# One decoder layer on one core: norm sums partly on TensorE, paired units in another order, fifth unit's weights ahead of stores, memory keys k by k

## The chip, the cores and the metric

One core of one Trainium2 chip runs the kernel. The metric is the device time of one execution in microseconds (us), as the median of three executions. Engines are named as in the profile: PE is TensorE, DVE is VectorE, ACT is ScalarE, POOL is GpSimd, SP is SyncE (which only issues DMAs here).

## The reference, cut to what matters

```python
x = x + 0.5 * swiglu(rmsnorm(x, ffn1_norm), ffn1_w_gu, ffn1_w_down)   # FFN1
h = rmsnorm(x, mix_norm)
z = h @ w_in                     # u, v | c_q, c_kv, k_rope | q_mem | three gates
y_a = spatial_gating(u, v, ...)                        # branch A
y_b = mla(c_q, c_kv, k_rope, ...)                      # branch B, causal attention
y_c = memory_attention(q_mem, mem, mem_norm, mem_w_kv, ...)   # branch C
x = x + sum_i(sigmoid(gate_i) * (y_i @ w_branch_i)) @ w_out
x = x + 0.5 * swiglu(rmsnorm(x, ffn2_norm), ffn2_w_gu, ffn2_w_down)   # FFN2

def swiglu(x, w_gu, w_down):
    g, u = split(x @ w_gu, 2)
    return (silu(g) * u) @ w_down

def memory_attention(...):       # in it, 256 memory tokens, 4 heads of 128:
    kv = rmsnorm(mem, mem_norm) @ w_kv
    k = rmsnorm(kv[keys], k_norm); v = kv[values]
```

x has 1024 tokens of 1024 channels, the FFNs are 2816 wide, and everything is fp32.

## The kernel before, in words

All activations live with channels on the partitions and tokens on the free axis, in two halves of 512 tokens; eight chunks c of 128 channels make up the 1024 channels (`DT` is 8).

**Products.** Every fp32 product is made of three passes (`mm3`, lines 139 to 141 in the profile): operands are split into a high part (`whi` by a cast on ACT, L127) and a low part (`wlo` by a subtraction on DVE, L128), and PE runs high by high, one low by high, and the other. One product of a "unit" is four blocks j of three passes, so 12 matmuls of 128x512.

**Units of seven products.** The FFN's first layer and the gates are computed two 512-wide column blocks at a time by seven products in place of eight (class `Seven`; `SwiGLU` and `Gates` derive from it). From the activations it needs the operands `b11`, `b12`, `b21`, `b22` and their combinations `t1` to `t4`; from the weights `a11`, `a12`, `a21`, `a22` and their sums `s1` to `s4` (`sums`, four DVE additions L1229 to L1234). `weights` splits one pair of them: part "a" is a11 and a12, "s" is s2 and s1, "t" is s3 and s4, "l" is a22. In this order a unit runs a11·b11, s2·t2, a12·b21, s1·t1, s3·t3, s4·b22, a22·t4. DVE adds the results together (`add`, L1255), ACT applies silu (L1459) or sigmoid (L1407), and `gate` multiplies (L1455).

**Pairs.** Where the second half of the tokens is not yet normalized, two units f and g run together (`units`): first s3·t3 and s4·b22 of both, which need the first half alone; meanwhile the second half's norm is made; then a11·b11, a12·b21, s2·t2, s1·t1 of both and a22·t4 of each. This happens three times: at the start of FFN1 (units 1 and 2, behind a unit 0 whose products are computed row by row on raw fp32, L1498), before the gates (units 0 and 1) and in FFN2 (units 0 and 1). There PE, DVE and ACT follow the order in which the code is written (`manual_schedule`). The unit behind a pair (3 in FFN1, 2 elsewhere) and all later ones run in `unit`, where a scheduler places DVE's and ACT's instructions.

**Norms.** ACT squares a chunk (L1112, L1116 adds it up on DVE; L354 and L359 elsewhere); `token_sums` then sums over channels with matmuls of the running sum by a column of ones (L368), ten small DVE instructions take the root (`rms`, L149 to L167), and `turn` spreads it with four transposes (L380) for the DVE products of L1141 and L1145.

**Spill.** Finished hidden blocks are combined on POOL (L1589) and stored by SP's queue; the weights of unit f are fetched by SP's queue too (`fetch`), in program order with the stores.

**Memory branch.** `mem_kv` normalizes the memory tokens and makes k and v with 48 matmuls each; in between a "filler" gives PE products of branch A, 12 matmuls at a time. `head_norm` normalizes k (L657 to L663), `to_feature` transposes it (L413).

Of the kernel before, what the change touches and what calls it, by code (L numbers as in the profile page):

```python
# [8 lines left out]
F32 = mybir.dt.float32  # L9
# [7 lines left out]
P = 128  # L17
# [25 lines left out]
class Kernel:  # L43
# [82 lines left out]
    def split(self, hi, lo, src, eng=None):  # L126
        self.nc.scalar.copy(hi, src)  # L127
        return (eng or self.nc.vector).tensor_tensor(lo, src, hi.bitcast(F32), op=ALU.subtract)  # L128

# [232 lines left out]
    def token_sums(self, acc, late=False, bank=None):  # L362


        n = acc.shape[-1] // P
        b = (bank or self.bank)()[:, :n]
        for t in range(n):
            i = self.nc.tensor.matmul(  # L368
                b[:, t:t + 1], acc[:, t * P:(t + 1) * P], self.ones, start=True, stop=True)
            if late and t == 0:  # L370
                self.after(i, self.last)
        return b
# [47 lines left out]
    def latent(self, h):  # L420
# [10 lines left out]
        def c_q(hf):  # L431
            acc, cols = None, slice(hf * 512, hf * 512 + 512)
            for j, d in enumerate(cq):
# [6 lines left out]
                eps[:, hf * 4:hf * 4 + 4], self.token_sums(acc), EPS / QR, EPS * EPS, op0=ALU.mult, op1=ALU.add)  # L440
# [224 lines left out]
    def mem_kv(self, p, filler):  # L665
# [4 lines left out]
        with tc.tile_pool(name="memkv", bufs=1) as q:  # L670
# [3 lines left out]
            for _ in range(2):  # L674
                next(filler)
# [3 lines left out]
            next(filler)  # L679
            r = self.rms(self.token_sums(acc, late=True), ML // P, D)  # L680
            for _ in range(2):
                next(filler)
# [3 lines left out]
            next(filler)  # L686
            for part in range(2):
                next(filler)
                w = self.load(a["mem_w_kv"][part])
                ps = self.mm()  # L690
                for i in range(2):
                    for d in range(DT):
                        s = tuple(x[:, d, i * P:(i + 1) * P] for x in mt)
                        self.mm3(ps[:, i], s, w[d], d == 0, d == DT - 1)
                if part == 0:
                    x = q.tile([P, 2, MH, MD], F32, name="m_k")
                    self.head_norm(x, [ps[:, 0], ps[:, 1]])
                    for hh in range(0, MH, 2):
                        self.to_feature(
                            tuple(t[:, hh:hh + 2].rearrange("p h m -> p (h m)") for t in kt),  # L700
                            [x[:, t, hh + k] for k in range(2) for t in range(2)], self.mk_g,
                        )
                else:
                    self.split(vv[0], vv[1], ps)
        return kt, vv

    def mem_attention(self, h, kt, vv, filler):
# [3 lines left out]
        with tc.tile_pool(name="mematt", bufs=1) as p:  # L711
# [4 lines left out]
            nc.vector.tensor_scalar(gq, self.mq_g, -scale, None, op0=ALU.mult)  # L716
# [75 lines left out]
    def attention(self):  # L792
# [15 lines left out]
        with tc.tile_pool(name="att", bufs=1) as p:  # L808
# [3 lines left out]
            nc.vector.tensor_scalar(gq[:QK], self.g_ev["q"], -scale, None, op0=ALU.mult)  # L812
# [154 lines left out]
    def project(self, merged, norm, sink):  # L967
# [3 lines left out]
        for half in range(2):  # L971
            for c in range(DT):
# [6 lines left out]
                norm.feed(half, c)  # L979
# [17 lines left out]
    def run(self):  # L997
# [12 lines left out]
        with tc.tile_pool(name="f1", bufs=1) as fp, self.banks("f1ps") as self.pm:  # L1010
# [7 lines left out]
            ffn.up(3)  # L1018
# [7 lines left out]
            def sink(half, c):  # L1026
                add = norm.square(half, c)
                keep(x1d, rows, half, c)
                return add
# [13 lines left out]
            with tc.manual_schedule(engines={E.PE, E.SP, E.DVE, E.Activation}):  # L1043
# [7 lines left out]
                    [do(gates.turned, 1)], late)  # L1051
                gates.units((0, 1), gates.w0)
# [4 lines left out]
        with tc.tile_pool(name="f2", bufs=1) as fp, self.banks("f2ps") as self.pm:  # L1057
# [10 lines left out]
            with tc.manual_schedule(engines={E.PE, E.DVE, E.Activation}):  # L1068
                ffn.units((0, 1))
            ffn.spill(0)  # L1070
            ffn.up(2)
# [21 lines left out]
class OpNorm:  # L1093
# [7 lines left out]
    def __init__(self, k, rows, gain, scaled=False):  # L1101
        self.k, self.x, self.t, self.gain, self.scaled = k, rows, rows, gain, scaled
        self.acc, self.r, self.s, self.op, self.rows = {}, {}, {}, {}, {}

    def feed(self, half, c):
        self.acc[half] = self.k.norm_feed(self.acc.get(half), self.x(half, c), 512)

    def square(self, half, c):
# [10 lines left out]

        return add  # L1120

    def tokens(self, half):
        k = self.k
        self.s[half] = k.token_sums(self.acc.pop(half), late=k.last is not None)
# [24 lines left out]
    def put(self, name, p, src, room=None):  # L1149

        k = self.k
        hi, lo = ((room or k.h4)(F32R) for _ in range(2))
        k.split(hi, lo, src)
        self.op.setdefault(name, {})[p] = (hi, lo)

# [40 lines left out]
class Seven:  # L1196
# [9 lines left out]

    def __init__(self, k, w, pool, norm):
# [10 lines left out]
    def fetch(self, f, rooms=None):  # L1218

        t = [room() for room in rooms or [self.k.x4] * 4]  # L1220
# [4 lines left out]
    def sums(self, f):  # L1225
# [10 lines left out]
    def weights(self, f, part):  # L1236

        k = self.k
        a1, a2, sa, sb = self.quad[f]
# [607 lines left out]
```

## Time and profile before

| | us |
|---|---|
| median of three executions | 2224.83 (2224.31 to 2226.88) |
| profiled execution, its own time | 2226.85 |
| span of the profiled execution | 2224.5 |
| PE busy in it | 2192.1 (99%) |
| DVE, ACT, POOL busy | 1552.2, 895.5, 260.3 |
| mean granted PE clock | 0.997 of full speed |

The span is the time from the first to the last recorded instruction; 2.35 us of the execution's own time lie around it. PE is busy in almost all of it, so that a stage is read by the moments in which PE waits and by the granted clock.

### The profile page before, as it was taken

What the parts mean: (1) busy time and instruction counts of PE and PEld (TensorE: products, weight loads), DVE (VectorE), ACT (ScalarE), POOL (GpSimd) and SP (SyncE); (2) the same over time, 40 slices, a digit from 0 to 9 for tenths busy, and PEclk for the clock granted to TensorE, in tenths of its full rate; (3) what the DMA queues carried; (4) which work ended last, traced back from release to release, by engine and by line L of the source; (5) the groups of instructions that cost most, each with busy time, mean ns of one, the idle gap of its engine ahead of it and who ended that gap; (6) DMA issues with size and microseconds to landing.
All of it is one profiled execution on the core that took longest, in us unless ns stands there. A gap on an engine that the chain in (4) does not pass through costs nothing.

```text
span 2224.5 us, 27605 instructions
## 1 busy us (share of the span) xinstructions
PE 2192.1 (99%) x10304; PEld 1823.2 (82%) x10304; DVE 1552.2 (70%) x2408; ACT 895.5 (40%) x1498; POOL 260.3 (12%) x250
## 2 busy tenths in 40 slices
PE   9899999999999999999999999999999999999999
PEld 5678888888887888888878889988878888888887
DVE  7866666579889555467565778885886666657784
ACT  5322222243445333444344548843432222224432
POOL 0111212100000000022000131140012121210000
PEclk9999999999999999999999999999999999999999
DMA  3332323285333333225151450074033333328542
GB/s 134 105 109 100 114 100 110 87 321 192 128 113 106 123 104 123 91 78 180 42 192 48 184 227 30 29 280 192 30 118 114 100 114 100 114 94 303 180 128 104
DMA packets 113062, 285.92 MB, mean 129 GB/s; under 512 B 13344, under 2 KB 21664, under 8 KB 112800
## 3 DMA queue, kind: packets, MB, share of 16 engines
q1 hardware_dynamic: 112928, 284.16, 36.7%
q8 instruction: 81, 1.33, 0.2%
q14 instruction: 53, 0.43, 0.1%
HBM read 201.80 MB, written 82.31 MB: 128 GB/s over the span
## 4 chain that ended last, share of the span: by engine, by line
PE 87%; DVE 9%; ACT 1%; DMA 1%; issue 1%; SPq 0%; DVEq 0%; ACTq 0%
PE one L141 13%; PE one L139 13%; PE one L140 13%; PE bank L139 12%; PE bank L141 12%; PE bank L140 12%; PE mm L139 3%; PE mm L140 2%; PE mm L141 2%; DVE wlo L128 2%; PE bank L871 1%; PE bank L413 1%; DVE h L128 1%; PE bank L886 1%; PE bank L887 1%
## 5 line engine op out<-in xcount | busy, mean ns | idle before, releaser
L127 ACT CAST whi<-x 128x1024 fp32r<-128x1024 f32 (+1 forms) x193 | 181.7, 945 | 476.4 <-PE one L140 207.9
L1255 DVE TENSOR_TENSOR t<-t,one 128x512 f32<-128x512 f32 x178 | 122.3, 687 | 237.2 <-PE one L141 236.9
L128 DVE TENSOR_TENSOR wlo<-x,whi 128x1024 fp32r<-128x1024 f32 (+1 forms) x193 | 231.8, 1204 | 38.4 <-ACT whi L127 38.2
L139 PE MATMUL bank<-h,whi 128*128 128x512 f32 x644 | 251.5, 391 | 0.0
L141 PE MATMUL bank<-h,wlo 128*128 128x512 f32 x644 | 250.9, 390 | 0.5 <-DVE wlo L128 0.5
L140 PE MATMUL bank<-h,whi 128*128 128x512 f32 x644 | 251.0, 390 | 0.0
L127 ACT CAST whi<-w 128x1024 fp32r<-128x1024 f32 (+1 forms) x136 | 120.0, 898 | 169.1 <-PE one L140 66.4
L139 PE MATMUL one<-h,whi 128*128 128x512 f32 x476 | 186.0, 391 | 1.9 <-ACT t L1342 1.0
L141 PE MATMUL one<-h,wlo 128*128 128x512 f32 x476 | 185.6, 390 | 1.4 <-DVE wlo L128 1.4
L140 PE MATMUL one<-h,whi 128*128 128x512 f32 x476 | 185.2, 389 | 0.0
L128 DVE TENSOR_TENSOR wlo<-w,whi 128x1024 fp32r<-128x1024 f32 (+1 forms) x136 | 138.9, 1033 | 62.8 <-ACT whi L127 59.0
L141 PE MATMUL one<-w,wlo 128*128 128x512 f32 x392 | 153.6, 392 | 2.9 <-DVE wlo L128 2.9
L139 PE MATMUL one<-w,whi 128*128 128x512 f32 x392 | 153.6, 392 | 2.9 <-DVE t L1255 2.0
L140 PE MATMUL one<-w,whi 128*128 128x512 f32 x392 | 153.2, 391 | 0.0
L141 PEld LDWEIGHTS bank<-h,wlo 128*128 128x128 f32 x644 | 121.1, 188 | 26.2 <-DVE wlo L128 0.9
L140 PEld LDWEIGHTS bank<-h,whi 128*128 128x128 f32 x644 | 121.2, 188 | 24.9
L139 PEld LDWEIGHTS bank<-h,whi 128*128 128x128 f32 x644 | 121.2, 188 | 24.9
L1589 POOL TENSOR_TENSOR raw<-raw 128x512 f32<-128x512 f32 x42 | 69.8, 1661 | 598.3 <-DVE raw L1455 598.2
L139 PE MATMUL bank<-whi 128*128 128x512 f32 x352 | 136.9, 389 | 0.0
L140 PE MATMUL bank<-wlo,whi 128*128 128x512 f32 x352 | 136.9, 389 | 0.0
L141 PE MATMUL bank<-whi,wlo 128*128 128x512 f32 x352 | 136.9, 389 | 0.0
L1589 POOL TENSOR_TENSOR w<-raw 128x512 f32<-128x512 f32 x43 | 84.8, 1987 | 228.0 <-DVE raw L1455 228.0
(374 smaller groups left out, 4996.3 us busy)
## 6 DMA issues: line engine op xcount, KB each, us to landing
x<-in_ffn_w_gu_dram SPq DMA_DIRECT2D x78, 512.0 KB, 5.1
w<-tdt SPq DMA_DIRECT2D x40, 512.0 KB, 4.4
tdb<-raw SPq DMA_DIRECT2D x66, 256.0 KB, 2.1
h<-in_ffn_w_down_dram SPq DMA_DIRECT2D x64, 256.0 KB, 6.1
w<-tdb SPq DMA_DIRECT2D x30, 512.0 KB, 4.5
gate<-raw SPq DMA_DIRECT2D x24, 512.0 KB, 2.6
tdt<-w SPq DMA_DIRECT2D x44, 256.0 KB, 2.0
tdt<-raw SPq DMA_DIRECT2D x42, 256.0 KB, 2.8
```

The lines of the kernel that those rows point to most:

```text
L127: self.nc.scalar.copy(hi, src)
L128: return (eng or self.nc.vector).tensor_tensor(lo, src, hi.bitcast(F32), op=ALU.subtract)
L139: mmul(out, s[0], m[0], start=first, stop=False, **kw)
L140: mmul(out, s[0], m[1], start=False, stop=False, **kw)
L141: self.last = mmul(out, s[1], m[0], start=False, stop=last, **kw)
L413: nc.tensor.transpose(b[:m, k * P:(k + 1) * P], s, self.ident)
L871: nc.tensor.transpose(b[:, at:at + P], prs[t][:, kk * P:(kk + 1) * P], self.ident)
L886: nc.tensor.matmul(o, w, pt[0], start=n == 0, stop=False)
L887: nc.tensor.matmul(o, w, pt[1], start=False, stop=n == len(pts) - 1)
L1255: return self.nc.vector.tensor_tensor(out, x, y, op=ALU.add)
L1589: sub = lambda d, x, y: nc.gpsimd.tensor_tensor(d, x, y, op=ALU.subtract)
```

## The change

Six things are done.

1. `token_sums` takes a list of accumulators. Squares that are marked `plain` are no longer added up on DVE; each gets four ones-matmuls of its own. This makes 2 more accumulators for FFN1's first half (chunks 6, 7), 4 for its second (4 to 7), 2 for the gates' second half (6, 7), and 1 for FFN2's (7).
2. In `units` the token sums stand after two of the four blocks of the first product, the turn after five blocks; some weight splits move behind them; the splits of a22 and t4 are all made ahead of the last reads; both a22·t4 stand together; and the gating (`then`) comes last.
3. The next unit's "a" part and its `sums` are prepared between (`ready`), and that unit is run in the same written order (`unit(f, True)`).
4. FFN1's start is written in another order, and `fetch(4)` stands ahead of the first spill's stores.
5. `mem_kv` spreads the filler as 2, 2, 2, 2, runs each product with d outside and i inside, and has the whole v product between `head_norm` and the transposes of k.
6. Two one-column multiplications (`m_gq`, `a_gq`) go from DVE to POOL.

```diff
     def token_sums(self, accs, late=False, bank=None):
...
         for t in range(n):
+            for m, acc in enumerate(accs):
+                i = self.nc.tensor.matmul(
+                    b[:, t:t + 1], acc[:, t * P:(t + 1) * P], self.ones, start=m == 0, stop=m == len(accs) - 1)
...
             def product(w):
                 ps = self.mm()
+                for d in range(DT):
+                    for i in range(2):
                         s = tuple(x[:, d, i * P:(i + 1) * P] for x in mt)
                         self.mm3(ps[:, i], s, w[d], d == 0, d == DT - 1)
+                return ps
+
+            ps = product(self.load(a["mem_w_kv"][0]))
+            w = self.load(a["mem_w_kv"][1])
+            x = q.tile([P, 2, MH, MD], F32, name="m_k")
+            self.head_norm(x, [ps[:, 0], ps[:, 1]])
+            ps = product(w)
+            for hh in range(0, MH, 2):
+                self.to_feature(
...
+            self.product(out, w[u], s, t, js=(j,))
+            if n == 1 and not known:
+                norm.tokens(1)
+                for p in fill[0]:
+                    more(*p)
+                norm.root(1)
+                for p in fill[1]:
+                    more(*p)
+            if n == 4 and not known:
+                norm.turn(1)
...
+        for u in fs:
+            self.mark = self.add(p1[u], p1[u], z[u])
+            self.emit(u, 1, 0, p1[u], y[u])
+        for u in fs:
             self.product(y[u], w[u], "a22", "t4", False)
-            self.emit(u, 0, 0, v2, x[u], v2)
         aside()
+        for then in [self.emit(u, 0, 0, p1[u], x[u], p1[u]) for u in fs]:
+            if then:
+                then()
...
             self.units(
+                (1, 2), w, (),
+                [lambda: keep(1), lambda: self.fetch(3, [k.x4] * 2), lambda: self.ready(3)])
             finish()
+            self.fetch(4, [k.x4] * 2)
+            self.spill(0, self.w4)
+            self.hid[3] = self.w4()
+            self.unit(3, True)
+            self.spill(1)
```

PE ahead of the gates, where s3·t3 of the first gate unit (`one` by `h`) runs and the second half's norm is summed. Before:

```order
L139 MATMUL one<-h_4895,whi 128x512
L140 MATMUL one<-h_4896,whi 128x512
L141 MATMUL one<-h_4895,wlo 128x512
L368 MATMUL bank<-ones,t 128x1 x4
L139 MATMUL one<-h_4782,whi 128x512
...
L141 MATMUL one<-h_4891,wlo 128x512
L380 MATMUL bank<-ident,rs_y 128x128 x4
L139 MATMUL bank<-h_4786,whi 128x512
```

Now (h_4913 is what h_4895 was, h_4800 what h_4782 was):

```order
L144 MATMUL one<-h_4804,whi 128x512
L145 MATMUL one<-h_4805,whi 128x512
L146 MATMUL one<-h_4804,wlo 128x512
L374 MATMUL bank<-ones,t 128x1 x12
L144 MATMUL one<-h_4913,whi 128x512
...
L146 MATMUL one<-h_4800,wlo 128x512
L386 MATMUL bank<-ident,rs_y 128x128 x4
L144 MATMUL one<-h_4800,whi 128x512
```

The sums (12 matmuls where 4 stood) moved ahead of the first product's second half, and the turn from behind the second product to its middle.

ACT at the end of FFN1's pair. The pair's silus write `t` (L1459, now L1498); the casts of unit 3's weights read `x4` tiles: whi_626 and whi_657 before, whi_632 and whi_677 now, are its parts "a" and "s". L1524, now L1565, is unit 0's silu. Before:

```order
L127 CAST x4_580<-x4_146 128x1024
L1459 ACTIVATE t_456<-t_456 128x512
L1459 ACTIVATE t_458<-t_458 128x512
L127 CAST whi_626<-x4_616 128x1024
L127 CAST whi_657<-x4_618 128x1024
L127 CAST whi_692<-x4_619 128x1024
L127 CAST whi_724<-x4_617 128x512
L1268 COPY t_676<-one_661 128x512
L1524 ACTIVATE t_296<-t_296 128x512
```

Now:

```order
L132 CAST x4_597<-x4_146 128x1024
L132 CAST whi_632<-x4_486 128x1024
L1498 ACTIVATE t_470<-t_470 128x512
L1498 ACTIVATE t_472<-t_472 128x512
L1565 ACTIVATE t_272<-t_272 128x512
L1565 ACTIVATE t_358<-t_358 128x512
L132 CAST whi_677<-x4_636 128x1024
L1297 COPY t_696<-one_681 128x512
L132 CAST whi_712<-x4_637 128x1024
```

Part "a" moved ahead of the pair's silus, and part "s" behind all four silus; on DVE the low part of "s" stands behind all the gating of the pair and of unit 0 in the same way.

PE in the memory branch, around the transposes of the normalized keys m_k (`mm` is the product of k or v, `bank` by `x` is a filler of branch A, `bank` by `h` the query rows). Before:

```order
L139 MATMUL mm<-whi,m_hi 128x512
L140 MATMUL mm<-wlo,m_hi 128x512
L141 MATMUL mm<-whi,m_lo 128x512
L413 MATMUL bank<-ident,m_k 128x128 x8
L139 MATMUL bank<-x_8265,whi 128x512
...
L141 MATMUL bank<-x_8271,wlo 128x512
L139 MATMUL mm<-whi,m_hi 128x512
```

Now:

```order
L144 MATMUL mm<-whi,m_hi 128x512
L145 MATMUL mm<-wlo,m_hi 128x512
L146 MATMUL mm<-whi,m_lo 128x512
L419 MATMUL bank<-ident,m_k 128x128 x8
L144 MATMUL bank<-whi,h_6714 128x512
L145 MATMUL bank<-wlo,h_6714 128x512
```

The eight transposes stood after 18 of v's 48 matmuls and now stand after all 48; the filler behind them went to the front, ahead of the memory norm's sums.

## Rows read from the trace of the kernel before

**Rows 1.** The page: PE's busy time, share of the span and instructions.

```profile
PE 2192.1 (99%) x10304; PEld 1823.2 (82%) x10304; DVE 1552.2 (70%) x2408; ACT 895.5 (40%) x1498; POOL 260.3 (12%) x250
```

**Rows 2.** Windows: length, busy us of each engine, PEclk, DMA share, GB/s.

```profile
0.00:125.00 125.00, 112.59 (x412) 78.20 (x413) 102.31 (x141) 57.67 (x78) 12.68 (x17) 0.96 0.35 123
660.00:720.00 60.00, 55.51 (x244) 44.12 (x243) 57.27 (x78) 31.27 (x38) 0.00 (x0) 1.00 0.30 99
1100.00:1167.00 67.00, 61.13 (x279) 48.96 (x278) 41.62 (x92) 27.45 (x55) 0.00 (x0) 0.97 0.51 175
1585.00:1660.00 75.00, 72.74 (x323) 59.02 (x322) 64.67 (x84) 30.63 (x37) 8.49 (x5) 1.00 0.29 95
```

**Rows 3.** PE's timeline in FFN1's start: start, us, instruction, [idle before it].

```profile
1.49 4.21 PE L206 MATMUL bank<-ident 128*128 128x128 f32 x18 [1.49 <-POOL ident masks.py:199]
...
80.54 0.50 PE L139 MATMUL bank<-x,whi 128*128 128x512 f32 x1 [1.88 <-DVE raw L1255]
81.84 0.63 PE L141 MATMUL bank<-x,wlo 128*128 128x512 f32 x1
82.27 0.63 PE L139 MATMUL bank<-x,whi 128*128 128x512 f32 x1
...
113.05 0.79 PE L141 MATMUL one<-w,wlo 128*128 128x512 f32 x1 [2.92 <-DVE wlo L128]
```

**Rows 4.** PE's timeline ahead of the gates.

```profile
667.20 0.39 PE L139 MATMUL one<-h,whi 128*128 128x512 f32 x1
667.88 0.39 PE L139 MATMUL one<-h,whi 128*128 128x512 f32 x1
...
669.33 1.05 PE L368 MATMUL bank<-ones,t 128*128 128x1 f32 x8
670.24 0.48 PE L139 MATMUL one<-h,whi 128*128 128x512 f32 x1
...
674.92 0.65 PE L380 MATMUL bank<-ident,rs_y 128*128 128x128 f32 x4 [1.67 <-DVE rs_y L160]
```

**Rows 5.** Windows at three places, columns as in rows 2.

```profile
700.00:710.00 10.00, 7.18 (x28) 4.48 (x26) 8.35 (x12) 3.84 (x5) 0.00 (x0) 1.00 0.34 107
115.00:117.50 2.50, 2.50 (x8) 1.92 (x7) 2.50 (x2) 0.00 (x0) 0.87 (x1) 0.50 0.44 138
1152.50:1155.00 2.50, 1.89 (x10) 1.79 (x11) 0.92 (x2) 0.91 (x2) 0.00 (x0) 0.70 0.22 82
1155.00:1157.50 2.50, 2.50 (x9) 1.99 (x7) 1.14 (x2) 0.46 (x1) 0.00 (x0) 0.61 0.00 0
1157.50:1160.00 2.50, 1.62 (x7) 0.79 (x5) 1.38 (x3) 1.14 (x2) 0.00 (x0) 1.00 0.00 0
```

**Rows 6.** DVE's timeline in FFN1's start.

```profile
60.88 2.35 DVE L128 TENSOR_TENSOR w<-x,w 128x1024 fp32r<-128x1024 f32 x2
63.15 2.35 DVE L1186 TENSOR_TENSOR x<-x,x 128x1024 f32<-128x1024 f32 x2
...
106.32 0.68 DVE L1229 TENSOR_TENSOR x<-x,x 128x512 f32<-128x512 f32 x1
106.92 0.68 DVE L1234 TENSOR_TENSOR x<-x 128x512 f32<-128x512 f32 x1
...
110.71 2.28 DVE L128 TENSOR_TENSOR wlo<-x,whi 128x1024 fp32r<-128x1024 f32 x1
```

**Rows 7.** ACT's groups, 1585 to 1660: count, busy us, mean ns, idle before.

```profile
L127 ACT CAST whi<-x 128x1024 fp32r<-128x1024 f32 x8 | 8.4, 1049 | 10.3 <-DVE x L1232 8.4 <-PE bank L140 1.2 <-DVE x L1233 0.7
L1459 ACT ACTIVATE t<-t 128x512 f32<-128x512 f32 x3 | 1.9, 631 | 3.7 <-DVE t L1255 3.7
```

**Rows 8.** POOL's timeline behind FFN1's first spill.

```profile
110.20 1.71 POOL L1589 TENSOR_TENSOR w<-raw 128x512 f32<-128x512 f32 x1
```

**Rows 9.** PE's timeline in the memory branch.

```profile
1122.82 0.58 PE L368 MATMUL bank<-ones,t 128*128 128x1 f32 x4 [1.51 <-DVE t L359]
...
1153.12 1.62 PE L413 MATMUL bank<-ident,m_k 128*128 128x128 f32 x8 [1.98 <-DVE m_k L663]
```

More of the change, by code (lines that the diff above doesn't have):

```diff
@@ L360, in norm_feed, with token_sums @@
         return acc
-    def token_sums(self, acc, late=False, bank=None):
-        n = acc.shape[-1] // P
+    def token_sums(self, accs, late=False, bank=None):
+        n = accs[0].shape[-1] // P
         b = (bank or self.bank)()[:, :n]
         for t in range(n):
[L368 to L371, printed above, removed]
+            for m, acc in enumerate(accs):
+                i = self.nc.tensor.matmul(
+                    b[:, t:t + 1], acc[:, t * P:(t + 1) * P], self.ones, start=m == 0, stop=m == len(accs) - 1)
+                if late and t == 0 and m == 0:
+                    self.after(i, self.last)
         return b
@@ L673, in mem_kv, with fill @@
             nc.sync.dma_start(x, a["mem"])
-            for _ in range(2):
-                next(filler)
+            def fill(n):
+                for _ in range(n):
+                    next(filler)
+            fill(2)
             acc = None
@@ L678, in mem_kv @@
                 acc = self.norm_feed(acc, x[:, c], ML, late=c == 0)
[L679 to L682, printed above, removed]
+            fill(2)
+            r = self.rms(self.token_sums([acc], late=True), ML // P, D)
+            fill(2)
             scale = self.norm_scale(r, late=True)
@@ L978, in project @@
                 nc.vector.tensor_tensor(x, x, b, op=ALU.add)
-                norm.feed(half, c)
+                norm.feed(half, c, half == 1 and c == DT - 1)
                 sink(half, c)
@@ L1026, in sink @@
             def sink(half, c):
-                add = norm.square(half, c)
+                add = norm.square(half, c, half == 1 and c >= DT - 2)
                 keep(x1d, rows, half, c)
@@ L1123, in tokens @@
         k = self.k
-        self.s[half] = k.token_sums(self.acc.pop(half), late=k.last is not None)
+        self.s[half] = k.token_sums(
+            [self.acc.pop(half), *self.plain.pop(half, ())], late=k.last is not None)
     def root(self, half):
@@ L1527, in finish @@
                 self.gate(0, 1 - half, gate[half])
-        def third():
-            self.fetch(3)
-            self.sums(3)
-            self.made[3] = self.weights(3, "a")
         with k.tc.manual_schedule(engines={E.PE, E.DVE, E.Activation, E.SP}):
```

218 lines of the change are left out of this document (109 added, 109 removed).

## The prediction, made before the changed kernel was timed

> **What bounds the kernel now.** The page comes first: PE is busy in 2192.1 of 2224.5 us [rows 1], so a change can win only the 32.4 us in which PE waits and what half clock costs, and whatever it adds to PE it must pay for. Then the windows, stage by stage, and in each row the reader takes length less PE busy, and the clock. FFN1's start (0 to 125) waits 12.4 us at a mean clock of 0.96; the gates' pair (660 to 720) 4.5; the memory branch (1100 to 1167) 5.9 at 0.97; FFN2's pair (1585 to 1660) 2.3 [rows 2]. That is 25 of the 32.4, and the change touches these four places; elsewhere PE's order is the same. Last, PE's timeline in each place, for what ended the wait: DVE almost every time, which in these stages does nearly all of what PE waits for (102.3 of 125 busy, 57.3 of 60) [rows 2]. So each stage is a race of DVE's queue against PE's products, and the order of DVE's queue decides.
>
> **Prices.** Three passes start 0.68 apart [rows 4], so 12 matmuls, one product, take 2.72 us; at half clock one matmul takes 0.43 in place of 0.227 [rows 3]. An accumulator's token sums hold PE from 669.33 to 670.24, 0.91 us [rows 4]. On DVE two 128x1024 instructions step 2.27, so 1.14 each, and a 128x512 one 0.60 [rows 6]. A 128x1024 cast on ACT takes 1.05, a silu 0.63 [rows 7].
>
> **The sums on PE.** 2 + 4 + 2 + 1 accumulators more, at 0.91, are 8.2 us of PE: 5.5 in FFN1's start, 1.8 ahead of the gates, 0.9 in FFN2. They take nine additions of 0.60 from DVE, 5.4 us. The row shows no cheaper price: a ones-matmul has one output column, and still each of the eight records costs 0.114.
>
> **The pair's order.** The earlier sums meet their aim: ahead of the gates the turn waits 1.67 for the root [rows 4], and now nine matmuls (2.0 us) stand between sums and turn, about as long as the ten small DVE instructions that make the root, so some 0.15 is left. The wait of the a22·t4 products is not removed. Both low parts of a22 and t4 (0.60 + 1.14 for the second unit) and the split of the "s" weights now stand on DVE ahead of the read that frees the first unit's bank. I followed DVE's queue from the norm on at the prices above: it frees the bank 2.35 us after PE has got there in FFN1, 2.3 in the gates and 1.1 in FFN2; s1·t1 waits another 0.5 in the first two.
>
> The new wait stands behind that, at the next unit's s2·t2. From the moment at which the bank is read, PE has a22·t4 of f and of g and a11·b11 to run, 36 matmuls or 8.2 us, and two passes more before it needs the low part. DVE has, ahead of that low part: two reads of g's banks 1.2, the low part of "a" 1.14, four weight sums 2.4, and the gating. In FFN1 the gating is eight 128x512 instructions for the pair, 4.8, and five for unit 0: two of 0.60, one of 1.14, two of 0.60, 3.5. ACT's high part stands behind two silus that need unit 0's first two: 1.2 + 1.14 + 2.4 + 4.8 + 1.2, then a silu 0.63 and the cast 1.05, 12.4. The low part ends at 1.2 + 1.14 + 2.4 + 4.8 + 3.5 + 1.14 = 14.2. PE so waits 4.2 for the one, runs two passes, and waits 1.35 for the other, **5.6 us**. In the gates there is no unit 0, but the cast of "a" stands behind a sigmoid that needs g's reads, so its low part ends at 1.2 + 0.7 + 1.05 + 1.14 = 4.1; four sums and four additions 4.8, a sigmoid, about as long as a silu, and the cast make 10.7, the low part 11.9: 2.5 and 0.75, **3.3 us**. In FFN2 no silu is late; the low part ends at 1.2 + 1.14 + 2.4 + 4.8 + 1.14 = 10.7, 8.65 are covered: **2.1 us**. Were "s" split ahead of the gating, all three would be nothing: reads, low part, sums, cast and split are 6.9, under the 8.2.
>
> **The fifth unit's weights.** PE waited 2.92 us at 113.05 [rows 3] behind weights that landed late, since their fetch stood behind a spill's stores on SP's queue; then the clock was at 0.50 [rows 5]. Ahead of the stores they no longer queue. The stores go out two transfers later, and what waits for them is POOL's next spill and no product; I cost that at nothing. If the cover is gone, the cost is the 2.92 of before. What would be late next are that unit's low parts on DVE, which by the same prices are done about 1 us before PE asks.
>
> **FFN1's start in all.** Before: 12.4 us of waits, and 0.04 of 125 us, 5.0, lost by the clock [rows 2]: 17.4. After: 1.5 at the very start that nothing touches [rows 3], 0.5 + 2.35 + 5.6, and 5.5 of sums, 15.5; the other early waits, about 3 us of DVE's, go since PE has the sums to do. Whether the clock falls again is read from the trace: it fell after waits of 1.88 [rows 3], 2.92 [rows 3, 5] and 1.98 [rows 5, 9], and not after 1.67 [rows 4]. A wait of 4.2 should drop it, for 12 matmuls or so at 0.2 more each: 2.4. Sum 17.9, **+0.5**, from -2 (clock holds, the early waits shrink) to +4 (POOL's spill stretches the low part, the clock falls twice).
>
> **Gates.** +1.8 of sums; waits 0.15 + 0.5 + 2.3 + 3.3 = 6.25 in place of 4.5; 10 us there had 2.8 of waits without a fall of the clock [rows 5], so I take half of a fall, 1.0; and some 1.4 us off for the slow restarts behind the many short waits that go. **+3.2**, from +1.5 to +6.
>
> **FFN2.** +0.9 of sums; waits 0.4 + 1.1 + 2.1 = 3.6 in place of 2.3; a third of a fall, 0.7. **+3.0**, from +1.5 to +5.
>
> **Memory branch.** Here the change moves the right thing. One filler more ahead of the sums, 2.7 us, covers their wait of 1.51; the eight transposes waited 1.98 for k's norm [rows 9] and now have the whole v product, 10.9 us, ahead of them. k's norm takes, from k's last matmul, the last cast 1.1, squares and copies 2.1, two reductions, the root and the last multiplication, with four low parts of query weights in its queue, about 9.5. Then the fall of the clock (0.70, 0.61) goes and the 0.88 behind it [rows 5]. With d outside, a weight block serves six matmuls in place of three, so weights are asked for at half the pace. Of the 5.9 us of waits 0.75 stay in branch A's mixing; 0.03 of 67 us is 2.0 of clock [rows 2]. **-7.1**, from -8 to -4 if v's weights, whose buffers come free with k's blocks, are late. The two multiplications on POOL are some tenths of a us off DVE, where it waits anyway: nothing.
>
> **Two rules beside the rows.** After a wait of 2.92 us PE ran at 0.50 for the next 2.5 us and longer [rows 3, 5]. The Trainium skill's page "TensorE: Matmul & The Clock Gate" (Part 1: The HAM clock gate) says the same: the throttled 1.2 GHz is the default, and only lasting activity earns 2.4 GHz. By it each of the three long waits that the change makes is paid a second time; that is rival (b). The rows are not of one mind: 2.8 us of short waits in 10 left the clock full [rows 5].
>
> DVE's low part took 2.28 us in place of 1.22 while POOL combined a spill, 1.71 [rows 6, 8]. In the Trainium skill, "SBUF — State Buffer" (SBUF: two separate sides) calls the port pair of the two "an exclusive lock, not a bandwidth split". In FFN1 the first spill starts just as the low part that PE waits for does. By the row that is 1.1 us more. By the page's lock it could be a whole POOL instruction, 1.7.
>
> **Sum.** +0.5 + 3.2 + 3.0 - 7.1 = -0.4 us against the span of 2224.5, so 2226.45 against that execution's own 2226.85 (2.35 lie around the span). That execution was 2.0 above the median of 2224.83; on the median's scale the forecast is 2224.4. A measurement tells apart about 0.2%, 4.4 us, here.
>
> **Rivals.** *(a) The waits are smaller than I count.* The clock holds through all three stages (-4.1), the early norms gain a further us. Then -0.4 - 5.1 gives 2219.3. For it speaks that the gates' 2.8 us left the clock alone; against it, that one wait in FFN1 alone is longer than any that the trace has. Chance 0.28.
> *(b) Next unit's s2·t2 decides.* PE stops there long enough that the clock falls fully in all three pairs (2.4 each where I took 2.4, 1.0 and 0.7: 3.1 more), and in FFN1 and FFN2 the spill stretches the low part that it waits for (1.1 each). -0.4 + 5.3 gives 2229.7; it decides from 4.8 us beyond my sum on. The fall behind 1.88 and 1.98 speaks for it. Chance 0.16.
> *(c) The memory branch does not pay.* k's norm and v's weights share DVE and SP's queue with branch A's stores; if the first v blocks come 2 us late, or the wait moves to the query rows, -7.1 becomes -2: 2229.5. Rows speak against it: DVE is busy 41.6 of 67 us there [rows 2]. Chance 0.10.
> The forecast itself, within 0.2% of before, has 0.46.
>
> **How the numbers follow.** Faster by over 0.2%: (a), 0.28. Within: 0.46. Slower: (b) and (c), 0.26. The range that leaves about a fifth out goes from 2218 (the stages' lower bounds -2, +1.5, +1.5 and -8 give -7) to 2231 (just beyond b and c).
>
> **What would show each step.** Right: a row of token sums of x24 and of x40 in FFN1; the turn ahead of the gates with under 0.4 us of wait; PE at the fourth unit's s2·t2 (`one` by `w`, L144) waiting over 4 us on ACT's cast, then on DVE's low part, and shorter copies of it in the gates and FFN2; no wait of 2.9 in the fifth unit; in the memory branch full clock, and transposes of m_k without a wait. Wrong: a next unit that starts s2·t2 unhindered would mean that I misread DVE's queue, and the time would be near 2215; transposes that still wait would mean that v's product covers less than I count.

## The result, and the profile after

The changed kernel takes 2231.18 us in the median of 14 runs (2227.56 to 2234.65), the kernel before 2225.64 in 14 runs beside it (2224.31 to 2228.19). The ratio is 1.0021, 95% interval [1.0013, 1.003]: some 4.7 us slower by the ratio and 5.5 by the medians. That is little, but the interval leaves out no change; 2224.4 was forecast. The profiled execution of the changed kernel has a span of 2228.1 us, 3.6 more than before, and the rest of this section asks where these 3.6 come from. (It took 2229.82 us, one of the faster ones of the changed kernel, and the one before 2226.85, so that the spans differ by less than the medians.)

The page, PE's line:

```profile
PE 2199.7 (99%) x10376; PEld 1834.7 (82%) x10376; DVE 1542.7 (69%) x2397; ACT 894.5 (40%) x1498; POOL 259.3 (12%) x252
```

PE is busy 7.6 us more than before [rows 1], DVE 9.5 less. The same four windows as before:

```profile
0.00:125.00 125.00, 115.53 (x445) 82.36 (x446) 93.06 (x128) 55.46 (x76) 12.19 (x19) 0.93 0.32 107
660.00:720.00 60.00, 56.54 (x252) 45.63 (x250) 52.40 (x72) 30.86 (x39) 0.00 (x0) 0.97 0.20 75
1100.00:1167.00 67.00, 65.72 (x314) 54.71 (x313) 42.90 (x95) 29.94 (x59) 0.00 (x0) 1.00 0.58 193
1585.00:1660.00 75.00, 68.96 (x305) 56.43 (x304) 59.08 (x78) 28.71 (x35) 7.61 (x5) 0.98 0.18 62
```

Against [rows 2], FFN1's start waits 9.5 us in place of 12.4, but at a clock of 0.93 in place of 0.96; the gates' pair waits 3.5 in place of 4.5, at 0.97 in place of 1.00; the memory branch waits 1.3 in place of 5.9 at full clock; FFN2's pair waits 6.0 in place of 2.3. For the share of each stage three marks are read that stand at the same work in both programs: the turn of the gates' first half, the token sums in the mixer, and the sums ahead of FFN2's second half. Before:

```profile
622.54 0.60 PE L380 MATMUL bank<-ident,rs_y 128*128 128x128 f32 x4
...
923.58 0.95 PE L368 MATMUL bank<-ones,t 128*128 128x1 f32 x8
...
1590.15 0.95 PE L368 MATMUL bank<-ones,t 128*128 128x1 f32 x8
```

After:

```profile
625.75 0.60 PE L386 MATMUL bank<-ident,rs_y 128*128 128x128 f32 x4
...
929.53 0.95 PE L374 MATMUL bank<-ones,t 128*128 128x1 f32 x8
...
1586.10 2.02 PE L374 MATMUL bank<-ones,t 128*128 128x1 f32 x16
```

FFN1's start cost 625.75 - 622.54 = +3.2 (forecast +0.5), the gates 303.8 - 301.0 = +2.7 (+3.2). The sums of FFN2 now stand six matmuls (1.36) earlier in the program, so the stretch with the memory branch gave 656.6 + 1.4 - 666.6 = -8.6 (-7.1), and what follows, to the ends of the spans, cost 642.0 - 1.4 - 634.35 = +6.3 (+3.0). Together +3.6. Two terms were far off: FFN1 and FFN2. The first two stretches as windows, before:

```profile
0.00:622.54 622.54, 610.13 (x2611) 490.23 (x2612) 452.22 (x636) 222.03 (x306) 78.54 (x53) 0.99 0.40 137
622.54:923.58 301.04, 296.55 (x1324) 244.54 (x1323) 199.42 (x264) 132.88 (x181) 0.00 (x0) 1.00 0.33 114
```

After:

```profile
0.00:625.75 625.75, 616.28 (x2658) 497.19 (x2659) 446.76 (x628) 222.07 (x306) 78.07 (x55) 0.99 0.40 136
625.75:929.53 303.78, 299.77 (x1340) 247.47 (x1339) 197.85 (x262) 132.47 (x181) 0.00 (x0) 0.99 0.33 113
```

Up to the first mark PE waits 2.9 us less and is busy 6.15 more; in the gates it waits 0.5 less and is busy 3.2 more.

FFN1's start, PE's timeline after (rows of the raw products L1539, of the sums L374, where a ones-matmul shows as two records, and the three long waits):

```profile
13.41 2.76 PE L374 MATMUL bank<-ones,t 128*128 128x1 f32 x24
16.03 5.38 PE L1539 MATMUL bank<-x,w 128*128 128x512 f32 x8
21.25 0.60 PE L386 MATMUL bank<-ident,rs_y 128*128 128x128 f32 x4
21.68 3.60 PE L1539 MATMUL bank<-x,w 128*128 128x512 f32 x8
...
33.70 4.83 PE L374 MATMUL bank<-ones,t 128*128 128x1 f32 x40
38.39 6.75 PE L1539 MATMUL one<-x,w 128*128 128x512 f32 x8
44.98 0.60 PE L386 MATMUL bank<-ident,rs_y 128*128 128x128 f32 x4
...
82.85 0.47 PE L144 MATMUL one<-x,whi 128*128 128x512 f32 x1 [1.95 <-DVE raw L1284]
95.89 0.80 PE L144 MATMUL one<-w,whi 128*128 128x512 f32 x1 [4.61 <-ACT whi L132]
97.97 0.80 PE L146 MATMUL one<-w,wlo 128*128 128x512 f32 x1 [0.85 <-DVE wlo L133]
```

The waits are nearly those forecast: 1.95 where 2.35 was worked out, 4.61 and 0.85 where 4.2 and 1.35 were, none in the fifth unit. What was not forecast is in the upper rows. Eight raw products take 3.44 us (21.68 to 25.12), but 5.22 behind the first sums (16.03 to 21.25) and 6.59 behind the second (38.39 to 44.98). No idle time stands ahead of them. The windows say why:

```profile
17.50:20.00 2.50, 2.50 (x4) 1.01 (x3) 2.33 (x7) 2.20 (x4) 0.00 (x0) 0.50 1.06 408
40.00:42.50 2.50, 2.50 (x4) 1.01 (x3) 2.26 (x9) 0.08 (x1) 0.00 (x0) 0.50 0.00 0
```

The clock is at half, behind PE that was busy all the time, but with matmuls of one column. These two falls cost 1.8 + 3.15 = 4.9 us. A third follows the long wait: the clock is at 0.50 from 97.5 to 100 too, and the twelve matmuls from 95.89 to 102.40 take 2.9 us longer than at full clock, the 0.85 of waiting left out.

The gates and FFN2's pair after, PE's rows that wait and the turn:

```profile
676.24 0.64 PE L386 MATMUL bank<-ident,rs_y 128*128 128x128 f32 x4
709.07 0.47 PE L144 MATMUL one<-x,whi 128*128 128x512 f32 x1 [1.98 <-DVE raw L1284]
720.03 0.50 PE L144 MATMUL one<-w,whi 128*128 128x512 f32 x1 [0.93 <-ACT whi L132]
721.29 0.50 PE L146 MATMUL one<-w,wlo 128*128 128x512 f32 x1 [0.53 <-DVE wlo L133]
```

```profile
1621.86 0.47 PE L144 MATMUL one<-x,whi 128*128 128x512 f32 x1 [1.78 <-DVE raw L1284]
...
1634.95 0.59 PE L146 MATMUL one<-w,wlo 128*128 128x512 f32 x1 [4.23 <-DVE wlo L133]
```

and what the last of them waited for, POOL's and DVE's rows of FFN2:

```profile
1630.88 2.93 POOL L1636 TENSOR_TENSOR w<-raw 128x512 f32<-128x512 f32 x2 [130.13 <-ACT t L1297]
...
1631.37 1.33 DVE L1494 TENSOR_TENSOR raw<-raw,t 128x512 f32<-128x512 f32 x1
1632.62 2.28 DVE L133 TENSOR_TENSOR wlo<-x,whi 128x1024 fp32r<-128x1024 f32 x1
```

The low part that unit 2 needs took 2.28 us beside POOL's spill, as the row of FFN1 before did [rows 6, 8], and the multiplication ahead of it 1.33. In the memory branch the transposes of k wait for nothing:

```profile
1163.68 1.04 PE L419 MATMUL bank<-ident,m_k 128*128 128x128 f32 x8
```

### The profile page after: what moved, and what is told of

It is laid out like the page before. It is cut to its first block, busy times and chain, and to the rows that moved or that the text cites. A ratio compares the mean times of both kernels' runs of the same rounds, so it can differ in the third digit from the quotient of the medians.

```text
span 2228.1 us, 27721 instructions
## 1 busy us (share of the span) xinstructions
PE 2199.7 (99%) x10376; PEld 1834.7 (82%) x10376; DVE 1542.7 (69%) x2397; ACT 894.5 (40%) x1498; POOL 259.3 (12%) x252
## 3 DMA queue, kind: packets, MB, share of 16 engines
q8 instruction: 81, 1.33, 0.2%
## 4 chain that ended last, share of the span: by engine, by line
PE 92%; DVE 5%; ACT 1%; issue 1%; DMA 0%; DVEq 0%; ACTq 0%
PE one L146 13%; PE bank L144 13%; PE one L144 13%; PE bank L146 13%; PE bank L145 13%; PE one L145 13%; PE mm L144 3%; PE mm L145 3%; PE mm L146 3%; PE bank L881 1%; PE bank L419 1%; PE bank L896 1%; DVE wlo L133 1%; PE bank L897 1%; PE one L1539 1%
## 5 line engine op out<-in xcount | busy, mean ns | idle before, releaser
L133 DVE TENSOR_TENSOR wlo<-x,whi 128x1024 fp32r<-128x1024 f32 (+1 forms) x189 | 226.7, 1204 | 33.5 <-ACT whi L132 33.5
L127 ACT CAST whi<-w 128x1024 fp32r<-128x1024 f32 (+1 forms) x108 | 95.1, 899 | 143.7 <-PE one L145 55.2
L128 DVE TENSOR_TENSOR wlo<-w,whi 128x1024 fp32r<-128x1024 f32 (+1 forms) x108 | 110.1, 1033 | 60.6 <-ACT whi L127 60.5
L1636 POOL TENSOR_TENSOR raw<-raw 128x512 f32<-128x512 f32 x39 | 64.1, 1645 | 593.4 <-DVE raw L1494 593.4
L128 DVE TENSOR_TENSOR wlo<-h,whi 128x512 fp32r<-128x512 f32 x130 | 88.1, 713 | 26.5 <-ACT whi L127 26.5
```

The lines of the kernel that those rows point to most:

```text
L133: return lambda: self.nc.vector.tensor_tensor(lo, src, hi.bitcast(F32), op=ALU.subtract)
L1636: sub = lambda d, x, y: nc.gpsimd.tensor_tensor(d, x, y, op=ALU.subtract)
```

## The experiments

Theory after the result: the memory branch and the fifth unit's fetch pay; the next unit's s2·t2 waits and, in FFN1, the blocks of one-column matmuls (by the clock) take it back. Rivals: the sums cost their PE time alone, or DVE's total work is the bound, so that a wait that goes in one place comes back in another. All ratios are against the kernel before, run beside each.

**1. The memory branch alone.** Before, with `mem_kv` of the change.

```diff
-                for i in range(2):
-                    for d in range(DT):
+                for d in range(DT):
+                    for i in range(2):
...
+            ps = product(w)
             for hh in range(0, MH, 2):
```

> The kernel before with the change's memory branch alone. In the changed kernel the shift against before falls from +5.95 us ahead of this branch to -2.7 behind it, some 8.6 us won. Theory (the memory branch pays in full, and the three pairs cost +3.2, +2.7 and +6.3): 2225.6 - 8.6 = 2217.0, ratio 0.996. Rival (the gain came from other parts that changed together with it, such as the pair ahead of FFN2 or the two multiplications moved to POOL): 2 us or less off, 2223 to 2226.

Measured: 2219.08, ratio 0.9966 [0.9953, 0.9979], so 7.6 us less. Its window of the branch reads like the changed kernel's:

```profile
1100.00:1167.00 67.00, 66.13 (x316) 55.05 (x315) 43.99 (x96) 29.99 (x59) 0.00 (x0) 1.00 0.55 187
```

The theory holds. This part is worth what was forecast, though the interval is wide (4.7 to 10.5 us).

**2. All sums back on DVE.** `feed(0, c)`, `feed(1, c)()`, `norm.square(half, c)`, `norm.feed(half, c)`: no square is plain.

```diff
-                feed(0, c, c >= 6)
+                feed(0, c)
...
-                feed(1, c, True)
+                feed(1, c)()
```

> The changed kernel with every square added up on DVE again, as before, and one accumulator in each token sum; the rest of the change stays. Theory (the sums cost PE 8.2 us of their own, and their blocks of one-column matmuls also drop the clock in FFN1's start, where the L1539 rows behind them took 1.8 and 3.2 us too long): PE gets back 8.2 + 5.0, DVE does nine additions of 0.60 more and so brings back 3 to 5 us of waits, 2231.2 - 9 = 2222, and FFN1's start shows no half clock at 17 and 38 us. Rival 1 (the sums cost their own time only, the clock falls there anyway): 2231.2 - 8.2 + 4 = 2227. Rival 2 (DVE's queue is the bound, so that each addition comes back as a wait): 2231 or more.

Measured: 2230.92, ratio 1.0021 [1.0012, 1.0029], the same as the changed kernel. The chain of waits and PE's rows at the second sums:

```profile
PE bank L374 <- DVE t L1132: 8.3, 4, 4.2
```

```profile
36.61 1.83 PE L374 MATMUL bank<-ones,t 128*128 128x1 f32 x8 [4.23 <-DVE t L1132]
38.30 5.61 PE L1539 MATMUL one<-x,w 128*128 128x512 f32 x8
```

PE got its 8.2 us back and waits 8.3 for the additions. Of the two falls in FFN1 the first is gone, but behind the wait of 4.23 the clock falls all the same (5.45 for eight raw products). Rival 2 was right here and my 2222 wrong: in these stages the sums on PE cost what they save.

**3. The next unit's s weights ahead of the gating.**

```diff
         self.sums(f, rooms)
+        d, self.low = self.weights_later(f, "s")
+        self.made[f] |= d
...
-        for then in [self.emit(u, 0, 0, p1[u], x[u], p1[u]) for u in fs]:
-            if then:
-                then()
+        thens = [self.emit(u, 0, 0, p1[u], x[u], p1[u]) for u in fs]
+        self.low()
         for u in fs:
             self.emit(u, 1, 1, v1[u], y[u])
...
+        for then in thens:
+            if then:
+                then()
```

> The changed kernel with the next unit's s weights split ahead of the pair's gating, in all three places: the cast in front of the pair's silus, the low part behind the two reads that free the first products' banks, then the reads of the last products, and the multiplications at the end. Theory (the s2-t2 waits of 5.46, 1.46 and 4.23 us, and the falls of the clock behind the first and the last, 3.06 and 1.70, come from that order alone): up to 15.9 us less, 2231.2 - 14 = 2217, with some of it lost to later bank reads. Rival (DVE's total of work is the bound in these stages, so that the wait only moves on, to a bank that the later gating reads or to the unit's t weights): 2228 to 2231, with new waits of 3 to 5 us a few products on.

Measured: 2221.07, ratio 0.9973 [0.9962, 0.9984], 10 us less than the changed kernel (14 were expected). In the gates and in FFN2 no wait is left at the next unit; in FFN1 another one stands there, and two of 1.06 and 0.97 behind it:

```profile
96.30 0.50 PE L144 MATMUL one<-h,whi 128*128 128x512 f32 x1 [2.46 <-ACT t L1298]
```

ACT's copy of unit 3's first product is behind two silus of unit 0, which wait for DVE. The order was the cause; of the 14 us some came back as new waits.

**4. The sums in fours.** FFN1's ones-matmuls are issued four at a time (one accumulator), each four followed by a row product, in place of 12 and 20 in a block.

```diff
-            rows(0, range(4))
-            norm.sums(0)
-            rows(0, (4, 5))
+            rows(0, range(3))
+            norm.some(0, 0)
+            rows(0, (3,))
+            norm.some(0, 1)
+            rows(0, (4,))
+            norm.some(0, 2, True)
+            norm.root(0)
+            rows(0, (5,))
...
```

> The changed kernel with the 12 and 20 ones-matmuls of FFN1's start no longer in two blocks: four at a time, each four between two row products, so that the same matmuls run in the same stretch. Theory (the two falls of the clock there, 1.8 and 3.2 us, come from PE doing nothing but one-column matmuls for 2.6 and 4.7 us): both go, 2231.2 - 5 = 2226. Rival (the falls come from what was ahead, such as the late loads, or from the fp32 row products themselves): the half clock stays in that stretch and the time is within 1.5 us of 2231.

Measured: 2234.86, ratio 1.0035 [1.0024, 1.0045]: no gain on the changed kernel, where 2226 was expected (the intervals of the two overlap). The windows show both halves:

```profile
17.50:20.00 2.50, 2.50 (x13) 1.56 (x12) 0.01 (x1) 2.32 (x4) 0.00 (x0) 1.00 1.06 406
37.50:40.00 2.50, 2.50 (x4) 0.97 (x3) 2.50 (x3) 1.30 (x2) 0.00 (x0) 0.51 0.01 3
```

In the first half the clock stays full. In the second I had put the first four ahead of their accumulator: PE waits 2.02 at 31.60 and the clock falls behind that wait. So this run decides nothing for the second half.

**5. The reads ahead of a22·t4.** On top of experiment 3:

```diff
-        for p, u in enumerate(fs):
-            low[u]()
-            t4[p]()
+        low[f]()
+        t4[0]()
         for u in fs:
             self.mark = self.add(p1[u], p1[u], z[u])
             self.emit(u, 1, 0, p1[u], y[u])
+            if u == f:
+                t4[1]()
+                low[g]()
```

> The kernel with the early s weights (e3_s_early) and one more move on DVE, in all three pairs: the two additions that read the first unit's banks ahead of a22-t4 stand behind the low parts of a22 and of t4's first half, and t4's second half, the second unit's a22 and its reads follow. Theory (PE's three waits ahead of a22-t4, 1.96, 1.98 and 1.78 us, are the two low parts of 0.60 and 1.14 ahead of the read, and the second one drops the clock): they shrink to 0.2 each and the gates' fall of 1.8 goes, 2221 - 6 = 2215. Rival (the same DVE work only moves the wait two blocks on, to the low part of t4's second half or to the second unit's bank): 2219 to 2222.

Measured: 2220.44, ratio 0.9966 [0.9954, 0.9979], by the ratios 1.6 us less than experiment 3, within both intervals. The chain of waits:

```profile
PE one L144 <- ACT t L1298: 3.6, 1, 3.6
PE one L144 <- DVE t L1284: 2.0, 2, 1.3
...
PE one L144 <- DVE raw L1284: 0.4, 2, 0.2
```

The three waits of 5.7 us in all became 0.4, but PE gets to the next unit so much earlier and waits there: 3.6 where it waited 2.5, and where it had not waited 0.96 and 0.53 in the gates and 1.3 in FFN2. The rival was right.

**6. Sums in fours where the accumulator is ready.** On top of experiment 5, with the first four behind four row products in both halves (once, in the second half, eight stand together).

```diff
-            rows(1, range(5))
-            norm.tokens(1)
+            rows(1, range(4))
+            for m in range(5):
+                norm.some(1, m, m == 4)
+                if m in (0, 1, 3):
+                    rows(1, (4 + (m + 1) // 2,))
...
```

> e5_reads with the ones-matmuls of FFN1's start in fours between row products, as in e4_spread, but with the first four placed where the accumulator is done by the trace (13.6 and 31.5 us), so that PE has no wait of 2 us that could drop the clock by itself. Theory (blocks of 12 and 20 ones-matmuls drop the clock): both falls there, 1.8 and 2.9 us, go, 4 us less than e5_reads. Rival (the clock falls there for another reason): half clock stays in 12 to 45 us and the time is that of e5_reads.

Measured: 2217.58, ratio 0.9957 [0.9944, 0.9969]. The window behind the second sums, of experiment 5 and of this one:

```profile
37.50:40.00 2.50, 2.50 (x7) 1.54 (x7) 2.27 (x9) 1.04 (x1) 0.00 (x0) 0.50 0.00 0
```

```profile
37.50:40.00 2.50, 2.50 (x14) 1.78 (x14) 2.50 (x3) 1.16 (x2) 0.00 (x0) 1.00 0.01 3
```

The same matmuls in the same stretch keep the full clock when they are spread. Over all five executions the mean granted clock is 0.998 or 0.999, where experiment 5 has 0.995 to 0.997. The time is 2 us less than experiment 5, within both intervals (4 were expected). Experiment 5's profile had no fall behind its first block, nor had those of experiments 11 and 12, though their code there is the changed kernel's, while experiment 3's had one: the first of the two falls comes and goes between executions.

**7. Blocks of sums, five times over.** Experiment 1 with each token sum computed five times into the same columns.

```diff
-        for t in range(n):
+        for m, t in ((m, t) for m in range(5) for t in range(n)):
```

> The kernel before with the changed memory branch (e1_mem_only, 2219), and every token sum made five times over into the same columns: blocks of 40 records where 8 stood, in six places, and of 20 where 4 stood in the memory branch. It only adds matmuls, with nothing else moved. By their own time, 32 records of 0.114 six times and 16 once, 23.7 us: 2243. Theory (a block of one-column matmuls of this length drops the clock with no wait ahead): half clock behind most of the x40 blocks, 2 to 3 us each, 2219 + 23.7 + 12 = 2255. Rival (they keep the clock; the falls in FFN1 had another reason): 2243 and full clock behind the blocks in the gates and in FFN2.

Measured: 2266.5, ratio 1.0176 [1.016, 1.0191]: 47 us above experiment 1. The sums stand in more places than I had counted: the pages have 272 records more (10576 against 10304), eight blocks of 40 and one of 20, which at 0.114 are 31.0 us of their own in place of 23.7. The gates' first half, PE's rows and the window behind:

```profile
623.58 4.52 PE L368 MATMUL bank<-ones,t 128*128 128x1 f32 x40
...
628.99 0.63 PE L139 MATMUL one<-whi 128*128 128x512 f32 x1
629.41 0.63 PE L140 MATMUL one<-wlo,whi 128*128 128x512 f32 x1
```

```profile
628.50:631.00 2.50, 2.50 (x7) 1.95 (x6) 2.19 (x11) 0.00 (x0) 0.00 (x0) 0.50 0.00 0
```

No wait stands ahead of the block, PE is busy 2.50 of 2.50, and the products behind it step 0.43 in place of 0.227. Windows of 20 or 25 us around the eight blocks of 40 records all show a clock of 0.80 to 0.93. In the profiled executions PE is busy 55.1 us longer than in experiment 1 (2241.0 against 2185.9), 24 more than the records themselves; it waits 5.2 less, which makes the 49.9 between the two spans. The mean clock of the run is 0.987 against 0.998, and 0.011 of 2264 us is 25, the same price. The theory is shown; its price I had put at half, 12.

**8. The fifth unit's fetch alone.** Experiment 1 with one line more:

```diff
             finish()
+            self.fetch(4)
             self.spill(0, k.x4)
```

> e1_mem_only with the fetch of the fifth unit's weights ahead of the first spill's stores, as in the change, alone. Theory (the wait of 2.92 us at 113 and the fall behind it, 2.97, come from the stores ahead of the fetch on SP's queue): 2219 - 5 = 2214. Rival (the weights come early and the low parts on DVE are late instead, beside POOL's spill): 2217 to 2220.

Measured: 2215.62, ratio 0.9946 [0.9934, 0.9959], 4.5 us less than experiment 1 by the ratios, whose intervals just overlap. The wait of 2.92 [rows 3], 2.78 in experiment 1, is gone; in its stead PE waits 1.77 a little earlier, for a bank that DVE frees:

```profile
106.66 0.50 PE L139 MATMUL bank<-x,whi 128*128 128x512 f32 x1 [1.77 <-DVE raw L1259]
```

The clock falls behind either wait. From the wait ahead of it (80.44 in experiment 1, 81.14 here) to the turn of the gates' first half the two profiles take 540.55 and 539.60 us, so that they show 1.0 of the 4.5 us; experiment 1's profile is of its fastest execution, and where the rest comes from is not shown. With the memory branch and one line of part 4, and the old order of the pairs, this version has the lowest median of all, though experiments 6, 9 and 10 overlap with it.

**9. Unit 0's gating behind unit 3's first copy.** Experiment 6, with `finish()` and the first spill called from `unit(3)` behind the copy.

```diff
+        if aside:
+            aside()
         self.product(x, w, "s2", "t2")
```

> e6_spread2 with unit 0's gating, the first spill and its stores moved behind the copy of the fourth unit's first product. In e6_spread2 that copy stands on ACT behind two silus that wait for unit 0's multiplications, so PE waits 3.6 us at 93.8 and then runs at half clock for 6 us. Theory (DVE's order around the next unit is what costs, and this is the last piece of it in FFN1): wait and fall go, 2217.6 - 3.6 - 2.5 = 2211.5. Rival (five multiplications of unit 0 in front of the fourth unit's reads only move the wait to s1-t1 or to the t weights): 2215 to 2218.

Measured: 2216.68, ratio 0.9958 [0.9945, 0.997]: nothing won. The 3.6 us on ACT are gone, and two waits for DVE's reads stand in their place:

```profile
95.49 0.80 PE L144 MATMUL one<-w,whi 128*128 128x512 f32 x1 [2.87 <-DVE t L1296]
104.70 0.50 PE L144 MATMUL one<-h,whi 128*128 128x512 f32 x1 [1.41 <-DVE t L1296]
```

DVE is busy 12.33 of 12.50 us from 87.5 to 100: in this stretch its queue has next to no time free, so that another order only moves the wait.

**10. Sums of the gates and FFN2 back on DVE.** Experiment 9, with plain squares in FFN1 only.

```diff
-                add = norm.square(half, c, half == 1 and c >= DT - 2)
+                add = norm.square(half, c)
...
-                norm.feed(half, c, half == 1 and c == DT - 1)
+                norm.feed(half, c)
```

> e9_finish_late with the extra squares of the gates and of FFN2 added up on DVE again (three additions of 0.60), so that PE has 2.7 us less to do there; FFN1's sums stay on PE, spread. Theory (what PE gives for the sums it gets back in waits of the same length, as FFN1 and the gates showed when all sums went back to DVE): within 1.5 us of e9_finish_late. Rival 1 (PE is the bound, so its 2.7 us are won): 2.7 less. Rival 2 (the waits for the root come back in full, 1.7 and more): 2 us more.

Measured: 2215.76, ratio 0.9954 [0.994, 0.9968], 0.9 us off experiment 9 by either measure, as the theory had it. The time alone could not tell this from 2.7 us less; the traces can: PE's waits are 2.4 us longer in all, most of it for the last addition.

```profile
PE bank L374 <- DVE t L1132: 2.2, 2, 1.3
```

**11. FFN2's first spill later in the code.**

```diff
-                ffn.spill(0, ffn.w4)
                 ffn.unit(2, True)
+                ffn.spill(0, ffn.w4)
```

> The changed kernel with FFN2's first spill behind unit 2 in place of ahead of it. In the changed kernel the low part that unit 2's s2-t2 waits for took 2.28 us beside POOL's first two combinations, and 1.22 elsewhere. Theory (POOL stretches it, 1.1 of the 4.23 us of that wait): the low part takes 1.2 us, the wait is 3.1 us, and the time 1 to 2 us less, 2230. Rival (the low part is long for another reason): it stays at 2.28 and the time is the same.

Measured: 2230.54, ratio 1.002 [1.0011, 1.0029], and the low part still 2.28. The edit moved nothing: POOL's instructions are not held by the order of the code there, and the spill started 1.7 us ahead of the low part as ever. It tells nothing of the theory.

**12. The spill held back by data.** POOL first copies a column of unit 2's s2·t2 sum into the tile that it then fills. The copy waited until that sum had been overwritten at the end of unit 2, at 1655 us, later than I meant.

```diff
+            nc.gpsimd.tensor_scalar(ta[:, 0, :1], behind[:, :1], 1.0, None, op0=ALU.mult)
         sub(t1, b12, b11)
```

> The changed kernel with FFN2's first spill behind unit 2's s2-t2: POOL's first combination writes a column that it first filled from the sum of that product, so that it can't start earlier (in e11_spill_late it started at the same moment as ever, 1.7 us ahead of the low part). Theory (POOL stretches the low part that PE waits for): it takes 1.2 us in place of 2.28, PE's wait there is 3.1 in place of 4.23, and the time 1 to 2 us less than the changed kernel. Rival (that low part is long for another reason): it stays at 2.28 and the wait at 4.2.

Measured: 2232.25, ratio 1.0027 [1.0017, 1.0037]. The rows of DVE and PE:

```profile
1630.55 1.22 DVE L133 TENSOR_TENSOR wlo<-x,whi 128x1024 fp32r<-128x1024 f32 x1
...
1631.83 0.50 PE L146 MATMUL one<-w,wlo 128*128 128x512 f32 x1 [2.50 <-DVE wlo L133]
```

```profile
1665.43 0.50 PE L144 MATMUL one<-h,whi 128*128 128x512 f32 x1 [2.23 <-DVE t L1284]
```

Without POOL beside them the low part takes 1.22 and the multiplication ahead of it 0.69 in place of 1.33, and PE waits 2.50 in place of 4.23: the mechanism is shown. The time is no less; the spill now stands beside unit 3's work, where three of DVE's 128x512 additions take 1.64 to 1.78 in place of 0.68 and PE waits 2.23.

## Why the prediction was wrong, step by step

**FFN1's start, +0.5 against +3.2: the step on the clock failed.** The prediction took the waits from 12.4 to 9.95, added 5.5 for the sums, priced at their matmuls alone, and took the clock's loss from 5.0 to 2.4, one fall behind the wait of 4.2. The waits came out at 9.5 and the sums at 5.6 (blocks of 2.62 and 4.69 us where 0.92 and 0.81 stood). But what is left of PE's busy time did not fall by 2.6, it grew by 0.6 (610.13 + 5.6 against 616.28): a miss of 3.2, of which the waits gave back 0.5. The two blocks of sums drop the clock themselves, 4.9 us in this execution, and the fall behind the long wait took 2.9: 7.8 us where 2.4 was put. Experiments 4 and 6 (spread, full clock) and 7 (blocks without any wait, half clock) show it. Against the 5.0 of before these 7.8 would be +2.8 and not +0.6; fewer slow restarts behind short waits may have given the rest back, but no run shows that. The trade of sums against additions was also no gain: experiments 2 and 10.

**FFN2, +3.0 against +6.3: the size of s2·t2's wait.** Mechanism and place were right, the size 2.1 where 4.23 was measured. From PE's start behind the bank's read (1621.86) to the end of the low part DVE's queue took 13.0 us where I counted 10.7. 1.7 of the difference is POOL's spill, which stretched the low part and the multiplication ahead of it: with the spill held back the same work took 11.3 (experiment 12, 1620.43 to 1631.77). I had put it into rival (b) alone, at 1.1, and not into the sum. The rest is steps of up to 0.78 where 0.60 was counted. Then the clock fell fully (1.7) where a third of a fall was priced, and a22·t4 waited 1.78 in place of 1.1. This is rival (b) in this one stage.

**The gates, +3.2 against +2.7: right in sum by luck, not in parts.** The waits were to grow by 1.75 and shrank by 0.5; the clock and the restarts together were to take off 0.4 and cost 1.4. a22·t4 waited 1.98 (2.3 counted). The clock fell there fully (0.84 from 709 to 720), and so PE came late to s2·t2 and waited 1.46 in place of 3.3. Where the same code kept its clock there, in experiment 11 (1.00 from 709 to 719), s2·t2 waited 2.52 and 0.53, near the forecast. The turn waited for nothing, where 0.15 was forecast.

**The memory branch, -7.1 against -8.6, and the fifth unit:** right; experiment 1 has the branch alone, and rival (c) fell. The fifth unit waits for nothing in the changed kernel, as forecast; what its earlier fetch is worth alone is less sure (experiment 8).

**The whole.** The sum was -0.4 and became +3.6. Rival (b) named 2229.7 and the deciding place; its condition came true in FFN2 only, and the clock behind the blocks of sums, which no rival had, made up the rest. Experiment 3 gives the order of s against the gating 10 us.

**Is the new order worth it when mended?** Experiments 3, 5, 6, 9 and 10 take 0.9973 to 0.9954; experiment 8, with the old order, takes 0.9946. Their intervals overlap. So neither order of the pairs is shown to be better. In FFN1 each wait that was taken away came back, in good part, at a later read (experiments 3, 5 and 9); in the gates the wait at s2·t2 went with experiment 3 and was back with experiment 5 (0.96 and 0.53), and in FFN2 1.3 us stood then where 4.23 had stood.

## What to carry to other kernels

Work that is moved to TensorE to spare another engine should be priced with what it does to the clock behind it, and many tiny matmuls may be better placed a few at a time between products, as experiment 6 has them. Where the next stage's operands stand in the same in-order queue as this stage's finishing work, put first what the next stage needs first, and count what other engines do to it at that moment. Two small parts of a large change, made alone, gave as much as any version with all of it: make each part alone before judging the whole.

## What the runs showed of the hardware that was not expected

A PE that never waits can lose its clock: behind 40 records of one-column matmuls in 4.4 us, with PE busy 2.50 of 2.50, the clock was at 0.50, the 1.2 GHz level, in experiment 7, and eight raw products took 6.59 us in place of 3.44 in the changed kernel. The Trainium skill's page "TensorE: Matmul & The Clock Gate" (Part 1: The HAM clock gate) puts the gate down to how busy PE has been recently. These rows do not agree with it as far as busy means the busy time of the profile: PE had no idle time there, and the clock fell all the same. The same code did it in one execution and not in another: behind the first block it fell in the changed kernel and in experiment 3, and not in experiments 5, 11 and 12. The changed kernel also has the wider spread, 2227.56 to 2234.65 us, and its mean granted clock goes with it, 0.995 in the fastest execution and 0.993 in the slowest; that this is the block's doing is not shown.

POOL's 128x512 combinations stretched DVE's work on operands in SBUF beside them: a 128x1024 low part took 2.28 us in place of 1.22 and a 128x512 multiplication 1.33 in place of 0.69, and both were back at the shorter time when experiment 12 moved the combinations away.
